# A hybrid decoder layer on one core: VectorE, ScalarE and SyncE held to the program's order, with work moved between chunks and the attention's probabilities turned by DMA

## The chip, the cores and the metric

The kernel runs on one core of a Trainium2 chip. The metric is the device time of one execution in microseconds, from repeated runs. One execution was profiled; its trace gives the start and length of every instruction on TensorE (PE, with its weight loads as PEld), VectorE (DVE), ScalarE (ACT) and GpSimd (POOL), and of the DMAs, which SyncE (SP) issues for the most part.

## The reference

One layer over 256 tokens of width 2048, in float32. What matters of it:

```python
hn = rmsnorm(h, norm_mix_w)
q, k, v, g_ret, xr, yr, g_a, g_b = split(hn @ w_in)
ret_out = silu(g_ret) * head_groupnorm(chunkwise_retention(rotary(q), rotary(k), v))   # 8 heads
xr = causal_dwconv(xr, rnn_conv_w, rnn_conv_b)                                       # 4 taps
rnn_out = gelu(yr) * rg_lru(xr, ...)       # gates by 16 small products, then a scan over tokens
merged = sigmoid(g_a) * (ret_out @ w_proj_ret) + sigmoid(g_b) * (rnn_out @ w_proj_rnn)
h = h + merged @ w_mix_out
# cross-attention over 256 memory tokens, 4 heads of 512
p = softmax((rmsnorm(h) @ w_q) @ (rmsnorm(mem) @ w_k).T * 512 ** -0.5)
h = h + (p @ (rmsnorm(mem) @ w_v)) @ w_o
# gated feed-forward, 3-tap causal convolution on 2 x 5632 channels
gate, val = split(causal_dwconv(rmsnorm(h) @ w_up, conv_w, conv_b))
h = h + (silu(gate) * val) @ w_down
out = rmsnorm(h, final_norm_w)
```

## The kernel before, in words

**Weights in chunks.** All weight matrices are laid out in one array in the order of their use. A chunk is up to four k-tiles of 128 rows by 512 columns (1 MB). `prefetch` loads a chunk into one of three `raw` buffers (SP, L244) and splits it in two halves of two k-tiles: ACT casts the high part `hi` (L269) and DVE subtracts it to get the low part `lo` (L270). There are six `hi` and six `lo` buffers, three chunks' worth. Each float32 product is three float32r matmuls: high by high, low by high, high by low. In `steps_n` a chunk is 24 matmuls of 512 columns; `chunks` keeps two chunks split ahead (`AHEAD`), so that the split of chunk c+3 is written after the matmuls of chunk c and before those of chunk c+1. It reuses chunk c's buffers.

**Work due after a chunk.** Everything that is not a weight matmul is hung on the chunks. `later(n, fn)` puts a function on a list, and `chunks` runs it n+1 chunks on, right behind that chunk's matmuls (called the boundary of the chunk below). A block of 512 output columns takes four chunks. Behind its last chunk come its drains: `turned_rows` scales the result from PSUM (DVE, L404, or L402 without a scale), and `by_dma` turns it so that features lie on partitions: ACT writes two planes of 16-bit words (L380, `pl`), SP issues two DMA transposes (L382, `pt`), and `join`, due `wait`+1 chunks later, puts the words together again (ACT, L391, `f`) and calls the function that uses them.

**The order.** The matmuls are pinned to the order of the program (`mm`, L206, and `turn_small`, L209, call `keep_in_program_order`). The instructions of ACT, DVE and SP are not: a planner orders each engine's queue by priority and by when it reckons an instruction to be ready. `high_priority` moves drains and planes forward.

**The stages, in time.** Two groups of retention (q, k, two v and two gate blocks each; rotary tables and rotations between; then per head scores, values and group norm, and `normalise` after the fourth head). Four blocks of the recurrent branch: an xr block, turned, joined and convolved by `conv_x` (ACT L763, DVE L765, three per tile), then a yr block whose join calls `gelu_y`; `recur` runs in two halves `RG_WAIT` chunks after the convolution: small products, four activations per tile (L730 to L733), and in the second half a square root (L745, which needs another activation table, as the next tanh at L787 does), a product (L746) and four scans (L748); `split_pair` (L423, L424) makes the parts for the next product. Then the gated projections, the mix-out, the attention (per head a key and a query block, `softmax`; `transpose_probs` turns the probabilities on PE; then per head a value block and `attend`), the output projection, and eleven pairs of gate and value blocks with three groups of down projections. `finish` and `last_down` end it with the final norm.

## Time and profile before

| | |
|---|---|
| median of 3 runs | 2023.56 us (2022.26 to 2023.94) |
| the profiled execution | 2022.28 us, of which its span is 2020.5 us |
| granted PE clock, mean | 0.996 |
| busy: PE, PEld, DVE, ACT | 2002.3, 1666.2, 1264.3, 1246.0 us |
| matmuls of the weights (L206, `acc`) | 8648 of 9060 |
| casts L269, mean of one | 710 of 1.052 us |
| subtractions L270, mean of one | 710 of 1.223 us |
| planes L380, joins L391, mean of one | 114 of 1.05 us, 114 of 1.35 us |
| transposes L382, issue to landing | 3.1, 4.9, 7.3 us (least, median, most) |
| DMA | 421.99 MB, 209 GB/s |

Times are in microseconds from the first instruction unless a line says ns. A group of instructions is named by line, engine, operation, and the tiles it writes and reads. A bracket behind an instruction in the timeline is the time that its engine sat idle before it, and what ended that. Matmuls are pipelined and their ends are modelled, so neighbouring ones overlap in the rows; their starts are 0.227 us apart where PE runs without a gap. Two instructions that follow each other on ACT or DVE overlap a little too, so that a row of several is shorter than the sum of its means.

### The profile page before, as it was taken

The page shows a single profiled execution, that of the slowest core. Times are in us where ns is not written, and L with a number is a line of the kernel's source. Part 1 is how long each engine was busy: PE and PEld are TensorE (multiplying, and loading weights), DVE is VectorE, ACT ScalarE, POOL GpSimd, SP SyncE. Part 2 cuts the span into 40 slices and gives each one's busy share as a digit, 9 for nine tenths or more (in the row PEclk, how much of TensorE's full clock was granted, in tenths as well). Part 3 has the DMA queues.
Part 4 walks back from the last instruction along what each step waited for, and adds up shares of the span by engine and source line. Part 5 has one row for each costly group of instructions (what it writes and reads, how often), then busy time and mean ns, then how long its engine had stood idle before and what let it go on. Part 6 is the DMA issues. An engine that isn't in the chain of part 4 may idle for free.

```text
span 2020.5 us, 23630 instructions
## 1 busy us (share of the span) xinstructions
PE 2002.3 (99%) x9060; PEld 1666.2 (82%) x9060; DVE 1264.3 (63%) x1563; ACT 1246.0 (62%) x1502; POOL 7.7 (0%) x12
## 2 busy tenths in 40 slices
PE   9999999999999999999999999999999999999998
PEld 7888888888888888788888888888888888888887
DVE  5856756888645555456555554567675577664675
ACT  6546547989434555478666556666774566644763
POOL 0000000000000000000000000000000000000000
PEclk9999999999999999999999999999999999999999
DMA  8665656665555566777766546667666566655663
GB/s 304 225 210 173 234 199 192 228 213 188 208 188 190 197 204 214 259 225 242 219 198 204 182 167 208 209 189 218 228 203 232 193 195 214 227 215 198 210 228 125
DMA packets 185153, 421.99 MB, mean 209 GB/s; under 512 B 127440, under 2 KB 132176, under 8 KB 139984
## 3 DMA queue, kind: packets, MB, share of 16 engines
q1 hardware_dynamic: 183520, 417.85, 62.2%
q10 hardware_dynamic: 1520, 2.63, 0.4%
q8 instruction: 71, 1.16, 0.2%
q14 instruction: 42, 0.34, 0.1%
HBM read 388.46 MB, written 2.10 MB: 193 GB/s over the span
## 4 chain that ended last, share of the span: by engine, by line
PE 97%; ACT 1%; DVE 1%; DMA 1%; issue 1%; SPq 0%; POOL 0%; POOLq 0%; DVEq 0%; ACTq 0%
PE acc L206 94%; PE sm L206 3%; DMA raw<-in_wall 1%; DVE lo L270 0%; ACT f L391 0%; DVE xr L765 0%; ACT pl L380 0%; ACT rows L653 0%; ACT hi L269 0%; POOL ro L507 0%; PE sm L209 0%; SPq L244 0%; DVE s L447 0%; ACT nat L1034 0%; DVE rows L404 0%
## 5 line engine op out<-in xcount | busy, mean ns | idle before, releaser
L206 PE MATMUL acc<-hi,s 128*128 128x512 f32 (+1 forms) x5680 | 1741.6, 388 | 4.2 <-ACT s L423 4.0
L270 DVE TENSOR_TENSOR lo<-raw,hi 128x1024 fp32r<-128x1024 f32 (+1 forms) x714 | 861.1, 1220 | 662.4 <-ACT hi L269 636.5
L206 PEld LDWEIGHTS acc<-hi,s 128*128 128x128 f32 x5680 | 1062.5, 188 | 222.1 <-ACT s L423 4.5
L206 PE MATMUL acc<-lo,s 128*128 128x512 f32 (+1 forms) x2840 | 1100.8, 388 | 2.0 <-DVE lo L270 2.0
L269 ACT CAST hi<-raw 128x1024 fp32r<-128x1024 f32 (+1 forms) x712 | 736.0, 1051 | 535.4 <-PE acc L206 466.7
L206 PEld LDWEIGHTS acc<-lo,s 128*128 128x128 f32 x2840 | 533.7, 188 | 111.6 <-DVE lo L270 2.7
L391 ACT COPY f<-pt 128x1024 uint16<-128x1024 uint16 x114 | 146.5, 1350 | 68.8 <-DMA pt<-pl 68.6
L380 ACT COPY pl<-rows 128x1024 uint16<-128x1024 uint16 x90 | 89.8, 1046 | 66.1 <-DVE rows L404 58.2
L404 DVE TENSOR_SCALAR rows<-acc,ro 128x512 f32<-128x512 f32 x68 | 47.8, 747 | 2.4 <-PE acc L206 2.4
L957 DVE SCALAR_TENSOR_TENSOR fv<-f,pf,fv 128x255 f32<-128x255 f32 (+1 forms) x88 | 35.8, 479 | 0.7 <-ACT fv L955 0.7
L957 DVE SCALAR_TENSOR_TENSOR fg<-f,pf,fg 128x255 f32<-128x255 f32 (+1 forms) x88 | 35.6, 478 | 0.0
L955 ACT ACTIVATE fv<-f,pf 128x256 f32<-128x256 f32 x44 | 22.9, 596 | 0.0
L955 ACT ACTIVATE fg<-f,pf 128x256 f32<-128x256 f32 x44 | 22.9, 594 | 0.0
L423 ACT ACTIVATE s<-fo 128x512 fp32r<-128x512 f32 x22 | 13.6, 635 | 14.1 <-DVE fo L977 14.1
L380 ACT COPY pl<-nat 128x1024 uint16<-128x1024 uint16 x16 | 16.0, 1046 | 9.6 <-DVE nat L835 9.6
L765 DVE SCALAR_TENSOR_TENSOR xr<-f,pa,xr 128x255 f32<-128x255 f32 (+2 forms) x48 | 20.1, 481 | 2.1 <-ACT xr L763 2.0
L446 ACT ACTIVATE s<-f,pb 128x256 fp32r<-128x256 f32 x48 | 20.4, 501 | 0.0
L447 DVE SCALAR_TENSOR_TENSOR s<-f,pb,s 128x256 fp32r<-128x256 f32 x48 | 19.9, 480 | 0.0
L206 PEld LDWEIGHTS sm<-s,s 128*128 128x128 f32 x144 | 18.8, 191 | 0.9
L206 PE MATMUL acc<-s,hi 128*128 128x512 f32 x64 | 17.6, 413 | 1.0 <-DVE hi L267 1.0
L206 PE MATMUL sm<-s,s 128*128 128x256 f32 (+1 forms) x144 | 18.6, 279 | 0.0
L421 DVE TENSOR_TENSOR s<-f,s 128x512 fp32r<-128x512 f32 x16 | 10.3, 687 | 10.0 <-ACT s L420 10.0
(154 smaller groups left out, 630.0 us busy)
## 6 DMA issues: line engine op xcount, KB each, us to landing
raw<-in_wall SPq DMA_DIRECT2D x352, 1024.0 KB, 4.9
raw<-in_wall SPq DMA_DIRECT2D x6, 512.0 KB, 6.4
nat<-in_x ACTq DMA_DIRECT2D x4, 512.0 KB, 8.2
nat<-in_x SPq DMA_DIRECT2D x4, 512.0 KB, 5.7
nat<-in_mem SPq DMA_DIRECT2D x4, 512.0 KB, 9.0
xt<-in_mem_t SPq DMA_DIRECT2D x8, 256.0 KB, 3.7
pt<-pl SPq DMA_TRANSPOSE x114, 4.9
xt<-in_x_t SPq DMA_DIRECT2D x7, 256.0 KB, 6.3
```

The source lines that it names most:

```text
L206: tc.keep_in_program_order(pe.matmul(*a, **k))
L269: act.copy(hi[:, ds], raw[:, cs, :])
L270: dve.tensor_tensor(out=lo[:, ds], in0=raw[:, cs, :], in1=hi[:, ds].bitcast(F32), op=ALU.subtract)
L380: act.copy(planes[:, :, h, :], words[:, h])
L391: act.copy(halves_[:, h], turned_[:, h])
L404: dve.tensor_scalar_mul(rows[:, tt, :], a[:, tt, :], r[:, tt : tt + 1])
L423: act.mul(t[:, :, 0:S], src, scale)
L446: act.activation(t[:, j, 0:S], src[:, j, :], AF.Identity, scale=wcol(j))
L447: dve.scalar_tensor_tensor(out=t[:, j, S:BW], in0=src[:, j, :], scalar=wcol(j), in1=t[:, j, 0:S].bitcast(F32), op0=ALU.mult, op1=ALU.subtract,
L765: dve.scalar_tensor_tensor(out=y[:, s:S], in0=z[:, 0 : S - s], scalar=p_cw(3 - s, t), in1=y[:, s:S], op0=ALU.mult, op1=ALU.add,)
L955: act.activation(y, z[:, j, :], AF.Identity, scale=pf[:, 2, t : t + 1], bias=pf[:, 3, t : t + 1])
L957: dve.scalar_tensor_tensor(out=y[:, s:S], in0=z[:, j, 0 : S - s], scalar=pf[:, 2 - s, t : t + 1], in1=y[:, s:S], op0=ALU.mult, op1=ALU.add,)
```

## The change

A small class passes every call on to an engine and pins the instruction behind everything that was written before it on that engine. PE, and from the end of the first q block on ACT, DVE and SP, are wrapped in it:

```diff
+class InOrder:
+    def __init__(self, tc, engine):
+        self.tc, self.engine = tc, engine
+    def __getattr__(self, name):
+        f = getattr(self.engine, name)
+        return lambda *a, **k: self.tc.keep_in_program_order(f(*a, **k))
...
+    pe = InOrder(tc, pe)
...
     qjoin = [joined(t, "q") for t in next(q_steps)]
     assert next(q_steps, None) is None
+    act, dve, sp = (InOrder(tc, e) for e in (act, dve, sp))
     later(0, tables)
```

The loads of the raw chunks are written where their buffer is read for the last time, right behind the split of the chunk three before:

```diff
+    def load(n):
+        while len(raws) < min(n, len(stream)):
...
+            raw = wp.tile([P, KC, BW], F32, tag="raw", bufs=RAW_BUFS, name=nm("raw"))
+            raws.append((raw, src))
+            if i >= 2 * len(EARLY):
+                sp.dma_start(out=raw[:, 0:nk, :], in_=src)
...
             ahead.append(((row, c), parts))
+            if i >= 2 * len(EARLY):
+                load(i + 1 + RAW_BUFS)
```

Work is moved between boundaries. The recurrence starts one chunk sooner (`RG_WAIT` 3 to 2) and the last gelu too. In `normalise`, the scaling and turning of the rows is put off to the next two boundaries. In `gelu_y` the two halves are interleaved and the product with the scan's result goes to the next boundary (`times_y`); the same is done with the last split of `gate_up`. In `residual` the turning comes before the squares, and the memory's sums of squares are spread over four boundaries:

```diff
-RG_WAIT = 3
+RG_WAIT = 2
...
+            def two_heads(i):
+                rows = big([P, 2, BW], s="rows")
+                for hh in (2 * i, 2 * i + 1):
...
+                        act.mul(rows[:, tt, c : c + DV], raws[hh][:, tt, :], rstd[:, hh, tt : tt + 1])
+                by_dma(rows, words.append, 4)
+            for i in range(2):
+                later(i, lambda i=i: two_heads(i))
...
+    def times_y(f, xr):
+        for pr in range(2):
+            o = tmp("rn")
...
+            dve.tensor_tensor(out=o, in0=xr[:, cs, :], in1=f[:, cs, :], op=ALU.mult)
+            rnn.append(split_pair(o, 0.5))
...
+            for y, y2, th in halves_:
                 act.activation(th, y2, AF.Tanh)
                 dve.scalar_tensor_tensor(out=y, in0=th, scalar=1.0, in1=y, op0=ALU.add, op1=ALU.mult)
+            later(0, lambda: times_y(f, xr[0]))
...
-        turned_rows(gemm_n("w_in", 0, xs, NT, O_YR + b * BW), rs0, gelu_y, 4 if b < 3 else 3)
+        turned_rows(gemm_n("w_in", 0, xs, NT, O_YR + b * BW), rs0, gelu_y, 4 if b < 3 else 2)
...
             dve.tensor_add(h, h, gemm_n(w, 0, st, NT, b * BW))
+            by_dma(hrow[b], lambda f, b=b: turn(f, b, out, wcol))
             squares(h, ss, b)
-            by_dma(hrow[b], lambda f, b=b: turn(f, b, out, wcol))
...
-                sum_squares(mnat[c], ss, c)
-            rsms.append(rstd_rows(ss))
+                later(c, lambda c=c: sum_squares(mnat[c], ss, c))
+            later(4, lambda: rsms.append(rstd_rows(ss)))
...
-            hid.append(split_pair(o, 0.5))
+            rows.append(o)
+        later(0, lambda: hid.extend(split_pair(o, 0.5) for o in rows))
```

The probabilities of two heads share one tile and are turned by `by_dma` when the second is done; the sixteen PE transposes and four copies from PSUM are gone:

```diff
-        later(1, lambda: transpose_probs(pr_))
+        if b % 2 == 1:
+            by_dma(probs[-1], lambda f: pTs.extend(f[:, 2 * i : 2 * i + 2, :] for i in range(2)))
```

More of the change, by code (lines that the diff above doesn't have):

```diff
@@ L203, in hybrid_layer @@
         pe.matmul(warm[:, 0, 0:P], ones, ones, start=True, stop=True)
-    def mm(*a, **k):
-        tc.keep_in_program_order(pe.matmul(*a, **k))
-    def turn_small(*a):
-        tc.keep_in_program_order(pe.transpose(*a))
+    pe = InOrder(tc, pe)
     plan = weight_plan()
@@ L226, in hybrid_layer @@
     at = [0]
+    raws = []
+    def load(n):
+        while len(raws) < min(n, len(stream)):
+            i = len(raws)
+            nk = stream[i][2]
+            size = nk * P * BW
+            src = wall[at[0] : at[0] + size].rearrange("(p k n) -> p k n", p=P, k=nk)
+            at[0] += size
+            raw = wp.tile([P, KC, BW], F32, tag="raw", bufs=RAW_BUFS, name=nm("raw"))
+            raws.append((raw, src))
+            if i >= 2 * len(EARLY):
+                sp.dma_start(out=raw[:, 0:nk, :], in_=src)
     def prefetch(n):
@@ L232, in prefetch @@
             taken[0] += 1
-            size = nk * P * BW
-            src = wall[at[0] : at[0] + size].rearrange("(p k n) -> p k n", p=P, k=nk)
-            at[0] += size
-            raw = wp.tile([P, KC, BW], F32, tag="raw", bufs=RAW_BUFS, name=nm("raw"))
+            load(i + 1)
+            raw, src = raws[i]
             k2 = row // (KH * P)
@@ L242, in prefetch @@
                 xs.load(k2 + 1)
-            for a, b in zip(cuts, cuts[1:]):
+            for a, b in zip(cuts, cuts[1:]) if early else ():
                 sp.dma_start(out=raw[:, a:b, :], in_=src[:, a:b, :])
@@ L329, in steps_t @@
                         a, sx = a[:, S:BW], sx[:, 0:S]
-                    mm(
+                    pe.matmul(
                         a, part, sx, start=k == 0 and t == 0, stop=k == nk - 1 and t == 0, skip_group_check=True
@@ L342, in products_n @@
         l = sx[:, S + tt * P : S + (tt + 1) * P]
-        mm(o, h, hi, start=start, stop=False)
-        mm(o, l, hi, start=False, stop=False)
-        mm(o, h, lo, start=False, stop=stop)
+        pe.matmul(o, h, hi, start=start, stop=False)
+        pe.matmul(o, l, hi, start=False, stop=False)
+        pe.matmul(o, h, lo, start=False, stop=stop)
     def steps_n(w, row, st, nk, col):
@@ L365, in product @@
         for i, (a, b) in enumerate(((l[0], r[0]), (l[0], r[1]), (l[1], r[0]))):
-            mm(o, a, b, start=start and i == 0, stop=stop and i == 2, skip_group_check=True)
+            pe.matmul(o, a, b, start=start and i == 0, stop=stop and i == 2, skip_group_check=True)
     def halves(t, j, cs=slice(0, S)):
@@ L478, in products @@
                 cs = slice(tt * P, (tt + 1) * P)
-                mm(bc[:, cs], ones, diag[:, cs], start=True, stop=True)
+                pe.matmul(bc[:, cs], ones, diag[:, cs], start=True, stop=True)
             act.copy(rsb, bc)
@@ L640, in normalise @@
         def normalise():
-            rows = [big([P, 2, BW], s="rows") for _ in range(2)]
             rstd = rsqrt_small(stats[:, :, 1], 8, 1.0, GN_EPS).rearrange("p (h t) -> p h t", t=2)
@@ L652, in normalise @@
                     )
-                    act.mul(rows[hh // 2][:, tt, (hh % 2) * DV : (hh % 2 + 1) * DV], y, rstd[:, hh, tt : tt + 1])
-            for i, r in enumerate(rows):
-                by_dma(r, words.append, 2 + i)
+            def two_heads(i):
+                rows = big([P, 2, BW], s="rows")
+                for hh in (2 * i, 2 * i + 1):
+                    for tt in range(2):
+                        c = (hh % 2) * DV
+                        act.mul(rows[:, tt, c : c + DV], raws[hh][:, tt, :], rstd[:, hh, tt : tt + 1])
+                by_dma(rows, words.append, 4)
+            for i in range(2):
+                later(i, lambda i=i: two_heads(i))
         for hh in range(4):
@@ L727, in recur @@
             for i in range(2):
-                mm(gp[:, i, :], rgw[:, i, j, :], xr[:, j, :], start=True, stop=True)
+                pe.matmul(gp[:, i, :], rgw[:, i, j, :], xr[:, j, :], start=True, stop=True)
             tr = tp.tile([P, S], F32, tag="tr", bufs=2, name=nm("tr"))
@@ L750, in recur @@
             )
+    def times_y(f, xr):
+        for pr in range(2):
+            o = tmp("rn")
+            cs = slice(2 * pr, 2 * pr + 2)
+            dve.tensor_tensor(out=o, in0=xr[:, cs, :], in1=f[:, cs, :], op=ALU.mult)
+            rnn.append(split_pair(o, 0.5))
     for b in range(4):
@@ L780, in gelu_y @@
         def gelu_y(f, xr=xr):
-            for pr in range(2):
-                y = f[:, 2 * pr : 2 * pr + 2, :]
-                y2, th = tmp("y2"), tmp("yt")
+            halves_ = [(f[:, 2 * pr : 2 * pr + 2, :], tmp("y2"), tmp("yt")) for pr in range(2)]
+            for y, y2, _ in halves_:
                 act.activation(y2, y, AF.Square)
@@ L786, in gelu_y @@
                 dve.tensor_tensor(out=y2, in0=y2, in1=y, op=ALU.mult)
+            for y, y2, th in halves_:
                 act.activation(th, y2, AF.Tanh)
                 dve.scalar_tensor_tensor(out=y, in0=th, scalar=1.0, in1=y, op0=ALU.add, op1=ALU.mult)
-            for pr in range(2):
-                o = tmp("rn")
-                cs = slice(2 * pr, 2 * pr + 2)
-                dve.tensor_tensor(out=o, in0=xr[0][:, cs, :], in1=f[:, cs, :], op=ALU.mult)
-                rnn.append(split_pair(o, 0.5))
+            later(0, lambda: times_y(f, xr[0]))
         turned_rows(gemm_n("w_in", 0, xs, NT, O_XR + b * BW), rs0, conv_x)
-        turned_rows(gemm_n("w_in", 0, xs, NT, O_YR + b * BW), rs0, gelu_y, 4 if b < 3 else 3)
+        turned_rows(gemm_n("w_in", 0, xs, NT, O_YR + b * BW), rs0, gelu_y, 4 if b < 3 else 2)
     def gated(c0, w, st, b, o):
@@ L870, in hybrid_layer, with softmax @@
     dve.tensor_scalar_mul(lscale, rstd_rows(ss1), float(XD**-0.5))
-    pTs, done = [], [0]
-    def softmax(q, k):
+    pTs, probs = [], []
+    def softmax(b, q, k):
         lg = small()
@@ L884, in softmax @@
         dve.scalar_tensor_tensor(out=nb, in0=mx, scalar=-1.0, in1=lscale, op0=ALU.mult, op1=ALU.mult)
-        pr_ = tmp("prob")
+        if b % 2 == 0:
+            probs.append(big([P, 2, BW], s="prob"))
+        pr_ = probs[-1][:, :, (b % 2) * S : (b % 2 + 1) * S]
         for tt in range(2):
@@ L893, in softmax @@
             dve.tensor_scalar_mul(pr_[:, tt, :], pr_[:, tt, :], rsm[:, tt : tt + 1])
-        later(1, lambda: transpose_probs(pr_))
-    def transpose_probs(pr_):
-        t = small()
-        for kt in range(2):
-            for tt in range(2):
-                turn_small(t[:, kt, tt * P : (tt + 1) * P], pr_[:, tt, kt * P : (kt + 1) * P], ident)
-        if done[0] == len(pTs):
-            two = tp.tile([P, 2, BW], F32, tag="sig", bufs=2, name=nm("pT"))
-            pTs.extend(two[:, i, :].rearrange("p (k s) -> p k s", s=S) for i in range(2))
-        pT = pTs[done[0]]
-        done[0] += 1
-        act.copy(pT, t)
+        if b % 2 == 1:
+            by_dma(probs[-1], lambda f: pTs.extend(f[:, 2 * i : 2 * i + 2, :] for i in range(2)))
     def split_block(f):
@@ L916, in query @@
             qs = split_block(f)
-            later(1, lambda: softmax(qs, ks))
+            later(1, lambda: softmax(b, qs, ks))
         turned_rows(gemm_n("xa_w_q", 0, h1s, NT, b * BW), None, query)
@@ L971, in gate_up @@
     def gate_up(gt, vl, hid):
+        rows = []
         for pr in range(2):
```

## The prediction

> **What bounds the kernel now.** I read the page's totals first, then the chain that ended last, then who TensorE (PE) waited for after the start, then the PE clock around the one long wait, then the timelines of the recurrent stage.

> ```profile
> span 2020.5 us, 23630 instructions
> PE 2002.3 (99%) x9060; PEld 1666.2 (82%) x9060; DVE 1264.3 (63%) x1563; ACT 1246.0 (62%) x1502; POOL 7.7 (0%) x12
> PE 97%; ACT 1%; DVE 1%; DMA 1%; issue 1%; SPq 0%; POOL 0%; POOLq 0%; DVEq 0%; ACTq 0%
> ```

> PE sets the time, and its stream is pinned already. One chunk of four k-tiles (24 matmuls) is this piece of the chain in order of time (start, length, what), 5.44 us without the last matmul's overhang:

> ```profile
> 300.96 5.47 PE acc L206 x24
> ```

> The waits of PE from 60 us to the end (total, times, longest) are two lines, 6.0 us. A fixed order can win those and little else:

> ```profile
> PE acc L206 <- ACT s L423: 4.0, 1, 4.0
> PE acc L206 <- DVE lo L270: 2.0, 1, 2.0
> ```

> A wait costs more than its length. The first matmuls after the long one, in the timeline, and the busy times of two stretches (length, then PE, PEld, DVE, ACT, POOL, then granted clock, DMA share, GB/s):

> ```profile
> 846.35 1.52 PE L206 MATMUL acc<-hi,s 128*128 128x512 f32 x2 [4.04 <-ACT s L423]
> ```
> ```profile
> 846.35:850.60 4.25, 4.25 (x9) 3.11 (x10) 1.27 (x2) 0.47 (x1) 0.00 (x0) 0.50 1.07 412
> 340.30:344.00 3.70, 3.69 (x16) 3.08 (x17) 2.22 (x2) 3.70 (x4) 0.00 (x0) 1.00 0.93 190
> ```

> After the 4.04 us wait the granted clock was 0.50 for 4.25 us, 2.1 us lost; after the 1.98 us wait, which ends at 340.3, it was 1.00. So I charge 2.1 us more for an idle above 4 us and nothing below 2. [...]

> The stage with least air on the other engines is the recurrent one (340 to 530 us: ACT busy 160.23 of 190 us, DVE 155.79). Its durations, here and below, from ACT and then DVE:

> ```profile
> 403.80 1.28 ACT L745 ACT_TABLE_LOAD   x1
> 405.09 1.06 ACT L745 ACTIVATE tt<-tt 128x1024 f32<-128x1024 f32 x1
> 407.95 1.99 ACT L380 COPY pl<-rows 128x1024 uint16<-128x1024 uint16 x2
> 423.74 2.56 ACT L391 COPY f<-pt 128x1024 uint16<-128x1024 uint16 x2
> 426.32 2.08 ACT L763 ACTIVATE xr<-f,pa 128x256 f32<-128x256 f32 x4
> 428.31 1.99 ACT L269 CAST hi<-raw 128x1024 fp32r<-128x1024 f32 x2
> ```
> ```profile
> 409.22 2.43 DVE L748 TENSOR_TENSOR_SCAN xr<-aa,ti 128x256 f32<-128x256 f32 x4
> 411.57 2.33 DVE L270 TENSOR_TENSOR lo<-raw,hi 128x1024 fp32r<-128x1024 f32 x2
> 421.37 1.29 DVE L792 TENSOR_TENSOR rn<-xr,f 128x512 f32<-128x512 f32 x2
> 428.27 1.41 DVE L404 TENSOR_SCALAR rows<-acc,ro 128x512 f32<-128x512 f32 x2
> 429.59 3.23 DVE L765 SCALAR_TENSOR_TENSOR xr<-f,pa,xr 128x253 f32<-128x253 f32 x8
> ```

> **The rule that the new order makes.** The split of chunk c+3 (casts L269, subtractions L270) is written behind everything due after chunk c. Its buffers come free as chunk c ends, and PE needs it two chunks later. Whatever is due at boundary c, with every hand-over between ACT and DVE, is now queued ahead of a split with 10.9 us of air. Before, the splits were slipped in between.

> **The recurrent stage, blocks 1 to 3.** Time 0 is the end of the xr block's last chunk. DVE comes late: the previous block's second recurrence half has its products 10.88 us earlier, and behind them stand eight activations (3.5), the table load (1.28), the square root (1.0), the product L746 (1.2), the scans (2.4) and two splits' subtractions (4.6), 14.05 with hand-overs, so DVE is free at 3.2. Then in order: rows L404 to 4.6; planes L380 to 6.6; casts of split 3 to 8.5; yr's join L391 to 11.0; squares to 12.1; table load to 13.4; two tanh to 14.6; casts of split 4 to 16.5; xr's join to 18.9; the first convolution step on ACT to 19.5; twelve L765 on DVE (0.395 apart) to 24.3; times_y, four hand-overs of about 0.65 between DVE and ACT, to 27.5; first cast of split 5 to 28.6, its subtraction 29.8. While ACT's scaling in times_y waits for DVE, the casts of split 5 stand behind it, and PE behind those. PE wants the split at 4 x 5.44 = 21.8: 6.85 us idle, 0.4 waiting for the subtraction, 2.1 at half clock. That is 9.3 a block, 27.9 for three. Bounds: ACT's own work in this stretch, with no hand-over at all, is 19.2 us and starts at 4.6, so it ends 2.0 past the deadline (2.9 with the subtraction, 8.7 for three); with no late DVE it would end in time. I take 27.9, since the hand-overs are real dependencies.

> **Other places, in time order,** each by the same adding of rows. Rotary tables, both q rotations and the first v split stand before split 12: ready at 66.2 and 67.45 instead of 61.0: 5.2 + 0.4 + 2.1 = 7.75. First retention group: the q join, a rotation and two_heads fall on one boundary, then the second rotation and a v split: 1.2 + 2.15 = 3.35. Same in block 0 of the recurrence: 0.2. Gelu of block 3, moved to wait 2, then times_y and the gate's tanh: 2.45. Softmax of head 3, two planes, the v split and a weight split all stand before attend(0)'s cast and subtraction, which PE needs at once: 4.6, with part of it cold 5.4 (4.6 to 6.7). Last block: finish(2)'s squares and products stand before the last split, 24 narrow matmuls of 0.12 ahead of need: 2.3. Together with the 27.9: 49.35. Each of these I let go down to half.

> **What goes.** The 4.04 us wait at 842 us with its 2.1: in the trace the join L391 (843.12) stands behind a cast that waits for PE (842.17); written order puts it ahead of an earlier split, and planes, then transposes landing in 3.2, then join and split end about 1 us in time. The 1.98 at 340 us, where spreading two_heads is what helps, and 0.38 at 930. The 16 PE transposes, 0.44 us per head on the chain: 1.76. Together 10.27.

> **What I cost at nothing.** The probabilities' new path adds four planes copies (1.05 each), four joins (1.35) and four transposes to SP (1.3 each) and drops four copies (0.58); head 1's and 3's planes sit before the drain at the same boundary, and without head 3 (counted above) the split behind still ends about 2 before PE's need. Raw loads are queued behind those transposes on SP, but each is issued as soon as its buffer is read, three chunks ahead (16 us against 4.9 to land). Squares moved behind the planes, sums of squares spread, words joined four chunks later: each 1.5 to 2.5 us on a boundary with over 2.5 spare. Feed-forward: a gate and value pair takes 43.5 us; with transposes complete about 6.5 and 4.7 us after the planes (the two values that alternate there, from the planes' end to the join), DVE's in-order loop is 43.4 long. That cover is thin: 1 us more of landing costs up to 2 us a pair once 2 to 3 us of slack are used.

> **Sum.** 49.35 - 10.27 = +39.1. The profiled run took 2022.28 (1.78 outside its span): 2061.4. The median of the runs is 1.28 above it: 2062.7, forecast 2062.

> **Rivals.**
> Faster: the three engines reach a boundary early, because most functions due there don't wait for PE, and every split is ready. Then only the 10.27 goes: 2013.3. Place: split 5 of each recurrent block; it decides from 28.6 coming down to 21.8. For it: at 842 the planner's own choice lost time, and ACT averages only 84% in this stage. Against: 19.2 us of ACT work alone miss the deadline by 2. Chance 0.15.
> Smaller: DVE is not late at xr's end, so each block loses 4.3 with no half clock (3 x 5.0 less): 2048. For it: half clock and lateness come from my chain alone. Against: scans and both splits are rows. 0.12.
> Feed-forward gives way: both transposes need 7.3 us, the longest landing seen, so each pair falls 3.3 us behind, 11 pairs, less 3 us of slack in each of three parts: +27, 2089. For: landings are 3.1 to 7.3, median 4.9. Against: DMA is busy 64% there, and SP gets its loads earlier. 0.14.
> Nothing changes because the planner's queues were in this order already: 2023.6. Against: L435 at 67.52 and 69.99 has two casts between, which written order forbids. 0.04.
> My forecast: 0.55.

> **How the numbers follow.** Low 2032: three blocks at 8.7 and the other places at half (10.7 of 21.45), less 10.27, is +9, or 2033; high 2090 takes in the feed-forward rival. That leaves out the faster and the unchanged cases, 0.19. A measurement here tells 0.2% (4 us) from none: faster 0.15, same 0.04, slower 0.81.

> **What would show it.** Right: PE waits for L269 and L270 appear, about 7 us long, three times at about 47 us distance in the recurrent stage, one near 61 us, one after the first v block of the attention; PEclk falls below 0.95 there; the wait at 842 is gone; ACT shows idle before L423 and L269 released by DVE L765 and L792. Wrong: PE idle in the recurrent stage under 5 us in all; or most of the new idle in the feed-forward part, behind DMA pt. A span within 4 us of 2020.5 with the waits moved would refute the sum, not the rule.

## The result, and the profile after

The changed kernel took 2077.1 us (median of 4 runs, 2075.0 to 2078.4), the kernel before 2023.4 us beside it: ratio 1.0265, 95% interval 1.0247 to 1.0283, 2.7% slower. The profiled execution took 2076.0 us with a span of 2074.2, 53.7 more than before.

The page of the changed kernel, its span, its busy times and its chain by engine. Every pinned instruction is recorded with the wrapper's line, L138, so groups must be told apart by their tiles:

```profile
span 2074.2 us, 23528 instructions
PE 2016.9 (97%) x9044; PEld 1670.2 (81%) x9044; DVE 1279.3 (62%) x1563; ACT 1241.8 (60%) x1506; POOL 8.3 (0%) x12
PE 83%; ACT 6%; DVE 5%; DMA 3%; issue 2%; SPq 0%; POOL 0%; POOLq 0%; ACTq 0%; DVEq 0%
```

PE's share of the chain fell from 97% to 83%; ACT and DVE now hold 11% where they held 2%, with almost the same work: DVE has the same 1563 instructions (busy 15 us longer in all), ACT four more (busy 4 us less). The four largest groups of waits of PE from 60 us to the end (total, times, longest) say for what:

```profile
PE acc L138 <- ACT hi L138: 32.1, 10, 7.6
PE acc L138 <- DVE lo L138: 4.9, 8, 1.0
PE sm L138 <- ACT ps L138: 4.5, 1, 4.5
PE sm L138 <- DVE ps L138: 3.0, 4, 1.0
```

`hi` and `lo` are the two parts of a weight split, `ps` the two parts of a head's probabilities, `sm` a small result in PSUM. The wait for `s` of 4.0 is gone, 45 us of others have come. The longest in PE's timeline (start of the work that follows the wait, its length, what, and in brackets the wait):

```profile
398.37 1.22 PE L138 MATMUL acc<-hi,s 128*128 128x512 f32 x2 [7.55 <-ACT hi L138]
454.57 1.22 PE L138 MATMUL acc<-hi,s 128*128 128x512 f32 x2 [7.19 <-ACT hi L138]
511.65 1.22 PE L138 MATMUL acc<-hi,s 128*128 128x512 f32 x2 [7.20 <-ACT hi L138]
1178.47 0.58 PE L138 MATMUL sm<-ps,v 128*128 128x256 f32 x1 [4.46 <-ACT ps L138]
2049.02 0.50 PE L138 MATMUL acc<-hi,s 128*128 128x256 f32 x2 [1.55 <-ACT hi L138]
```

The first three are recurrent blocks 1 to 3. Why ACT was late, in ACT's timeline of block 2:

```profile
429.48 2.00 ACT L138 COPY pl<-rows 128x1024 uint16<-128x1024 uint16 x2 [5.88 <-DVE rows L138]
...
443.88 2.08 ACT L138 ACTIVATE xr<-f,pa 128x256 f32<-128x256 f32 x4
450.97 0.63 ACT L138 ACTIVATE s<-rn 128x512 fp32r<-128x512 f32 x1 [5.01 <-DVE rn L138]
452.96 0.63 ACT L138 ACTIVATE s<-rn 128x512 fp32r<-128x512 f32 x1 [1.36 <-DVE rn L138]
453.49 3.87 ACT L138 CAST hi<-raw 128x1024 fp32r<-128x1024 f32 x4
```

ACT stands idle for 5.0 and 1.4 us in front of `times_y`, because DVE is at its twelve convolution steps. Behind it, at 453.49, are four casts of weights that wait for nothing but their turn. PE needed the first at 447.38. In the same stretch on DVE the convolution is one piece:

```profile
444.51 5.82 DVE L138 SCALAR_TENSOR_TENSOR xr<-f,pa,xr 128x255 f32<-128x255 f32 x12 [1.70 <-ACT xr L138]
```

Busy times of stretches (length, then PE, PEld, DVE, ACT, POOL, then granted clock, DMA share, GB/s) show what else a wait costs; the second row begins inside the wait that ends at 454.57:

```profile
340.00:540.00 200.00, 176.97 (x747) 143.83 (x746) 143.56 (x188) 151.32 (x201) 0.00 (x0) 0.93 0.59 182
449.40:459.70 10.30, 5.09 (x11) 3.59 (x12) 8.63 (x11) 5.03 (x6) 0.00 (x0) 0.50 0.14 48
```

In the recurrent stage PE lost 22.7 us of its 199.7, and the clock was 0.93; after this one wait 5.1 us of work ran at half clock, 2.6 us lost.

**Where the 53.7 us arose.** PE's matmuls into `acc` are the same 8648 in the same order in both kernels, so the delay of each one can be followed through the span, waits and clock together:

| place | predicted | measured |
|---|---|---|
| start of the kernel | 0 | -1.2 |
| rotary tables, first v split | +7.75 | +6.2 |
| first retention group | +3.35 | +6.4 |
| recurrence, block 0 | +0.2 | +1.1 |
| the wait at 340 | -1.98 | -1.98 |
| recurrence, blocks 1 to 3 | +27.9 | +30.2 |
| gelu of block 3 | +2.45 | +1.65 |
| the wait at 842 and its half clock | -6.15 | -6.5 |
| mix-out, 860 to 985 | -0.38 | +4.7 |
| 16 transposes of PE | -1.76 | -1.2 in three heads, the fourth in the next row |
| attend(0) | +5.4 | +7.45 |
| attend(1) to attend(3) | 0 | +2.7 |
| feed-forward | 0 | 0 |
| last block | +2.3 | +4.2 |
| sum | +39.1 | +53.7 |

### The profile page after: what moved, and what is told of

Read it like the earlier page. It is cut to its first block, busy times and chain, and to the rows that moved or that the text cites. A ratio compares the mean times of both kernels' runs of the same rounds, so it can differ in the third digit from the quotient of the medians.

```text
span 2074.2 us, 23528 instructions
## 1 busy us (share of the span) xinstructions
PE 2016.9 (97%) x9044; PEld 1670.2 (81%) x9044; DVE 1279.3 (62%) x1563; ACT 1241.8 (60%) x1506; POOL 8.3 (0%) x12
## 4 chain that ended last, share of the span: by engine, by line
PE 83%; ACT 6%; DVE 5%; DMA 3%; issue 2%; SPq 0%; POOL 0%; POOLq 0%; ACTq 0%; DVEq 0%
PE acc L138 81%; PE sm L138 2%; DVE lo L138 2%; ACT hi L138 2%; DMA raw<-in_wall 1%; DVE xr L138 1%; ACT f L138 1%; DMA nat<-in_x 1%; ACT pl L138 0%; DMA posi<-in_positions 0%; ACT tt L138 0%; ACT L138 0%; ACT s L138 0%; DVE nat L138 0%; DVE rows L138 0%
## 5 line engine op out<-in xcount | busy, mean ns | idle before, releaser
L138 PE MATMUL acc<-hi,s 128*128 128x512 f32 (+1 forms) x5680 | 1748.7, 389 | 32.7 <-ACT hi L138 32.1
L138 PEld LDWEIGHTS acc<-hi,s 128*128 128x128 f32 x5680 | 1066.7, 189 | 254.5 <-ACT hi L138 36.1
L138 PE MATMUL acc<-lo,s 128*128 128x512 f32 (+1 forms) x2840 | 1105.6, 389 | 5.2 <-DVE lo L138 4.9
L138 DVE TENSOR_TENSOR lo<-raw,hi 128x1024 fp32r<-128x1024 f32 x694 | 819.0, 1221 | 405.8 <-ACT hi L138 392.5
L138 ACT CAST hi<-raw 128x1024 fp32r<-128x1024 f32 x694 | 696.1, 1048 | 275.8 <-PE acc L138 257.4
L138 PEld LDWEIGHTS acc<-lo,s 128*128 128x128 f32 x2840 | 536.1, 189 | 121.1 <-DVE lo L138 11.2
L138 ACT COPY pl<-rows 128x1024 uint16<-128x1024 uint16 x90 | 89.7, 1044 | 169.1 <-DVE rows L138 168.9
L138 ACT COPY f<-pt 128x1024 uint16<-128x1024 uint16 x118 | 151.2, 1350 | 39.1 <-DMA pt<-pl 39.1
L138 DVE SCALAR_TENSOR_TENSOR fv<-f,pf,fv 128x255 f32<-128x255 f32 x88 | 39.6, 481 | 31.4 <-ACT fv L138 29.9
L138 DVE TENSOR_SCALAR rows<-acc,ro 128x512 f32<-128x512 f32 x68 | 47.8, 744 | 13.5 <-PE acc L138 13.4
L138 DVE SCALAR_TENSOR_TENSOR fg<-f,pf,fg 128x255 f32<-128x255 f32 x88 | 39.6, 482 | 26.1 <-ACT fg L138 24.5
L138 DVE TENSOR_TENSOR nat<-nat,acc 128x1024 f32<-128x1024 f32 (+1 forms) x23 | 24.9, 1080 | 46.7 <-PE acc L138 46.7
L138 ACT COPY pl<-nat 128x1024 uint16<-128x1024 uint16 x16 | 16.0, 1044 | 33.4 <-DVE nat L138 33.4
L290 DVE TENSOR_TENSOR lo<-raw,hi 128x1024 fp32r<-128x1024 f32 (+1 forms) x20 | 21.9, 1117 | 11.9 <-ACT hi L289 11.5
L138 DVE SCALAR_TENSOR_TENSOR s<-f,pb,s 128x256 fp32r<-128x256 f32 x48 | 20.2, 482 | 13.1 <-ACT s L138 13.1
L138 ACT ACTIVATE sig<-acc,half_rs 128x512 f32<-128x512 f32 x16 | 10.1, 685 | 29.9 <-PE acc L138 29.9
L138 DVE SCALAR_TENSOR_TENSOR xr<-f,pa,xr 128x255 f32<-128x255 f32 (+2 forms) x48 | 22.1, 482 | 6.2 <-ACT xr L138 5.1
L138 ACT ACTIVATE junk<-nat 128x512 f32<-128x512 f32 x30 | 18.6, 622 | 11.1 <-DVE nat L138 11.1
L138 ACT COPY pl<-m 128x1024 uint16<-128x1024 uint16 x8 | 8.0, 1044 | 28.5 <-DVE m L138 28.5
L138 DVE SCALAR_TENSOR_TENSOR v<-acc,ro,v 128x512 fp32r<-128x512 f32 x16 | 12.0, 750 | 20.9 <-ACT v L138 20.9
L138 ACT ACTIVATE prob<-sm,sx,lscale 128x256 f32<-128x256 f32 x8 | 4.5, 561 | 34.2 <-DVE sx L138 34.2
L138 DVE TENSOR_TENSOR s<-f,s 128x512 fp32r<-128x512 f32 x16 | 10.4, 689 | 22.3 <-ACT s L138 22.3
```

The costliest lines, as they stand in the source:

```text
L138: return lambda *a, **k: self.tc.keep_in_program_order(f(*a, **k))
L290: dve.tensor_tensor(out=lo[:, ds], in0=raw[:, cs, :], in1=hi[:, ds].bitcast(F32), op=ALU.subtract)
```

## The experiments

**Without the fixed order.** The changed kernel, less one line:

```diff
-    act, dve, sp = (InOrder(tc, e) for e in (act, dve, sp))
```

> The changed kernel without the pins on ACT, DVE and SP (PE stays pinned; loads, moved work and the turning by DMA stay). Theory A (the written order makes the waits: a split stands behind all that is due at its boundary): the three waits of about 7.2 us in the recurrent stage, the 3.7 us at 69 us and the 4.5 us at 1178 us go, PE idle after 60 us under 8 us in all, time 2010 to 2026. Rival B (the moved work or the probabilities' new path costs the time by itself): PE idle stays over 30 us, time over 2060. Rival C (the loads, now issued right behind a split, are what is late): the waits stay but fall to the raw transfers.

2031.7 us (2031.0 to 2032.8), ratio 1.0046 (1.0029 to 1.0063). So about 45 of the 53.7 us come from the fixed order of the three engines, and all three recurrent waits of 7 us are gone. The two largest groups of PE's waits from 60 us to the end:

```profile
PE acc L138 <- DVE lo L290: 5.3, 4, 2.0
PE acc L138 <- ACT s L445: 4.0, 1, 4.0
```

But the rest of the change is no gain either, 8.9 us slower than before: above the expected range. The place of it was followed in the same way: the 340 wait is gone, but two waits of 1.8 and 2.0 us for lo came near 380; the 4.04 us wait at 842 is still there; about 5 us arise at the first attend, about 3 in the feed-forward behind three waits (0.65 for `s`, 0.3 and 1.2 for lo). The wait at 842 is thus cured by the fixed order, not by the moved work. Why the two waits near 380 came stays open.

**The fixed order without the moved work.** The kernel before with the wrappers on all engines, and the early `load`, and nothing else of the change:

> The kernel before with the pins on PE, ACT, DVE and SP and the loads written behind the splits, and nothing else: no work moved, probabilities turned on PE. Theory A: worse than the changed kernel, since gelu and the product with the scan stand on one boundary and the recurrence one chunk later leaves DVE about 8.6 us late at the end of an xr block instead of 3.2: over 10 us of idle a block there, and the first retention group's normalise on one boundary; time 2085 to 2130. Rival B (the moved work costs the time): near 2024, at most 2035.

2123.8 us (2120.8 to 2124.8), ratio 1.0497 (1.0481 to 1.0513), inside the theory's range. The waits of PE from 60 us to the end:

```profile
PE acc L138 <- ACT hi L138: 48.3, 16, 6.8
PE acc L138 <- DVE lo L138: 15.2, 14, 3.0
```

Fixing the order costs 101 us on the old program, and the moved work takes 47 of them away again. As a whole the moved work is worth something only under the fixed order; in the planner's order (above) it and the probabilities together cost 9, though one part of it gains there, as a run below shows.

**The recurrence one chunk earlier still.**

```diff
-RG_WAIT = 2
+RG_WAIT = 1
```

> The changed kernel with the recurrence one more chunk earlier (RG_WAIT 1). Theory A says DVE comes 3.2 us late to an xr block's end because of the recurrence just before; one chunk earlier takes that away: idle before chunk 5 of recurrent blocks 1 to 3 falls from 7.2 to about 4 us each, and 1.7 us of small products may hide in it; time 2060 to 2069. Rival D (ACT's own load in this stretch is the bound, the late DVE does not matter): waits stay within 1 us of 7.2, time 2075 to 2079.

2078.2 us (2075.0 to 2078.9), ratio 1.0271 (1.0256 to 1.0286): no gain. The time is the rival's, but its sign is not there: it had the waits stay within 1 us of 7.2. DVE is no longer late: its rows now wait for PE. But the loss only splits in two; in PE's timeline of one block:

```profile
423.80 0.54 PE L138 MATMUL acc<-lo,s 128*128 128x512 f32 x1 [3.10 <-DVE lo L138]
457.27 0.73 PE L138 MATMUL acc<-hi,s 128*128 128x512 f32 x2 [3.09 <-ACT hi L138]
```

The next hi wait ends at 514.60, 57.3 us after this one; in the changed kernel the distance is 57.1 (511.65 less 454.57), in the kernel before a block takes 47.0 (the same two matmuls at 427.19 and 474.19). The chain that ended last lies wholly on PE over such a block of the kernel before. Over a block of the changed kernel (454 to 512 us) it lies on PE for 29% of the time, on ACT and DVE, in turn, for 65%; here (457 to 515) for 12% and 80%. So a chain of hand-overs between ACT and DVE sets most of the block's length, and in this placing it is as long as in the changed kernel.

**Two products one chunk later.** `times_y`, and `attend` of each head, come after the next split:

```diff
-            later(0, lambda: times_y(f, xr[0]))
+            later(1, lambda: times_y(f, xr[0]))
...
-        later(0, lambda b=b, v=v: attend(b, v))
+        later(1, lambda b=b, v=v: attend(b, v))
```

> The changed kernel with times_y one boundary later and attend one boundary later. Theory A: in the recurrent stage split 5 no longer stands behind the four hand-overs of times_y, but split 6 does: each of blocks 1 to 3 loses about 5 us instead of 10; at the attention the waits of 4.46 and 0.95 us and the three of 0.67 go, about 10 us; time 2044 to 2058. Rival D (ACT's load is the bound in the recurrent stage): the wait there only moves, 28 us and more stay in the three blocks; time 2065 to 2070.

2065.0 us (2063.5 to 2067.1), ratio 1.0210 (1.0194 to 1.0225): short of the theory's range by 7 us, at the lower end of the rival's. By the delays the recurrent stage with its last gelu got about 6 us back, the attention about 5. With `times_y` out of the way the cast came at 445.95, before PE needed it. The wait stayed, though, half as long, and changed sides (PE, then DVE):

```profile
451.61 0.79 PE L138 MATMUL acc<-lo,s 128*128 128x512 f32 x1 [3.83 <-DVE lo L138]
```
```profile
444.60 5.82 DVE L138 SCALAR_TENSOR_TENSOR xr<-f,pa,xr 128x255 f32<-128x255 f32 x12 [1.68 <-ACT xr L138]
450.33 2.35 DVE L138 TENSOR_TENSOR lo<-raw,hi 128x1024 fp32r<-128x1024 f32 x2
```

The subtraction of that split stands behind the convolution. Two queues have to be right for one split. A block takes 55.7 us here (this wait ends at 451.61, the next at 507.32): moving this piece shortens the chain by 1.4, not more.

**Which engine's queue?** The changed kernel with VectorE, and then with ScalarE, left to the planner:

```diff
-    act, dve, sp = (InOrder(tc, e) for e in (act, dve, sp))
+    act, sp = (InOrder(tc, e) for e in (act, sp))
```

> The changed kernel (2077.1 us) with VectorE left to the planner; ScalarE and SyncE stay in the program's order. Theory A (the 45 us of the fixed order come from the hand-overs between ScalarE and VectorE: a split needs a cast on the one and a subtraction on the other, and in a fixed order both stand behind a step that goes to and fro between the two, so both must be free before a split can pass it): ScalarE's casts still stand behind the two scalings of the recurrent block's product, so each of blocks 1 to 3 gets at most 1 to 2 us better; some of the tables and of attend(0) comes back: 2064 to 2077, and PE's waits in the recurrent stage stay over 4 us and are still for hi. Rival B (one engine's queue alone makes the loss, and it is VectorE's, which comes late into each recurrent block by about 3 us and runs the twelve convolution steps in one piece): nearly all 45 us come back: 2030 to 2045.

2057.1 us (2056.6 to 2058.0), ratio 1.0168 (1.0152 to 1.0183).

```diff
+    dve, sp = (InOrder(tc, e) for e in (dve, sp))
```

> The changed kernel (2077.1 us) with ScalarE left to the planner; VectorE and SyncE stay in the program's order. Theory A (both engines must be free before a split can pass): the casts can pass the scalings, but the subtraction of the same split stands on VectorE behind the twelve convolution steps and the products, so PE's waits in the recurrent stage turn from hi into lo and keep most of their length; what stands on ScalarE alone (tables, attend(0)) gets up to 8 us shorter: 2060 to 2075. Rival C (it is ScalarE's queue alone, the engine with the casts and all copies): 2030 to 2045.

2077.9 us (2076.3 to 2079.8), ratio 1.0270 (1.0255 to 1.0285). The wait of PE in block 2 in the two, VectorE free and ScalarE free:

```profile
441.12 0.79 PE L138 MATMUL acc<-lo,s 128*128 128x512 f32 x1 [4.03 <-DVE lo L290]
```
```profile
457.24 0.79 PE L138 MATMUL acc<-lo,s 128*128 128x512 f32 x1 [6.68 <-DVE lo L138]
```

Freeing ScalarE gives nothing: hi waits of 7.2 to 7.6 become lo waits of 6.7 to 8.3, since DVE's fixed order still holds the subtraction. Freeing VectorE gives 20 us, of which about 11 in blocks 1 to 3, and still leaves 4 us in each block. Both rivals in which one engine's queue makes the whole loss fall. The theory's own ranges were missed as well, by 3 us on ScalarE, which gains nothing at all, and by 7 on VectorE, which gains more: of the two, VectorE's order is the dearer. With VectorE free the theory also had the wrong half: it said that the waits would still be for hi, and they are for lo. ACT, then DVE, in block 2:

```profile
434.85 3.88 ACT L138 CAST hi<-raw 128x1024 fp32r<-128x1024 f32 x4
```
```profile
432.46 4.55 DVE L802 SCALAR_TENSOR_TENSOR xr<-f,pa,xr 128x255 f32<-128x255 f32 x11 [0.76 <-ACT xr L138]
439.84 6.90 DVE L290 TENSOR_TENSOR lo<-raw,hi 128x1024 fp32r<-128x1024 f32 x6
```

The first cast was done at 435.9, before PE wanted it; the planner itself laid the subtraction behind the convolution.

**The recurrent stage alone left to the planner**, on all three engines; the rest stays fixed:

```diff
+    act, dve, sp = nc.scalar, nc.vector, nc.sync
     for b in range(4):
         rgw = big([P, 2, 4, P], s="rgw")
...
+    act, dve, sp = (InOrder(tc, e) for e in (act, dve, sp))
     def gated(c0, w, st, b, o):
```

> The changed kernel (2077.1 us) with VectorE, ScalarE and SyncE left to the planner in the recurrent stage alone (from the first recurrent block to the gated products); everywhere else their order stays fixed. Theory A: the 30.2 us of blocks 1 to 3 and the 1 to 2 us of blocks 0 and 3 go, and the 3 us that the unpinned kernel lost near 380 come: 2046 to 2051. Rival I (the loss sits in what the change moved in this stage, the recurrence's wait of two and the products put off, not in the fixed order): 2065 to 2077.

2053.4 us (2049.0 to 2056.2), ratio 1.0150 (1.0137 to 1.0164), the median 2.4 above the range. The waits of 7 us in blocks 1 to 3 are gone, two for lo near 390 (1.97 and 2.00, as in the first experiment) have come; by the delays the stage gave 24 us back. So the fixed order, not the work that was moved in this stage, makes the loss there, and of these runs only the ones with both engines free undo it. SyncE was free in them too; its order alone was not tested, but between 380 and 515 us of the changed kernel ACT never waits for a load.

**The probabilities alone**, both ways round. First the changed kernel with PE's transposes back:

```diff
-        if b % 2 == 1:
-            by_dma(probs[-1], lambda f: pTs.extend(f[:, 2 * i : 2 * i + 2, :] for i in range(2)))
+        later(1, lambda: transpose_probs(pr_))
```

> The changed kernel (2077.1 us) with the attention's probabilities turned on TensorE again, as before; all else is kept. Theory A: attend(0)'s cast loses two planes copies (2.1 us) ahead of it, the 16 transposes on PE come back (1.76 us): 2076 to 2079, nothing that can be measured. Rival E (the way through the DMA is itself what makes attend(0) wait, 7.45 us here): the waits at 1178 and at the three attends after it go, 10 us less and 1.8 more: 2069.

2074.5 us (2073.5 to 2075.9), ratio 1.0254 (1.0238 to 1.0269): 2.6 us below the changed kernel, between the two expectations, but not clear of noise: the changed kernel's interval, 1.0247 to 1.0283, overlaps. In the profiled executions PE lost 7.4 us over the attention here, against the kernel before, and 8.4 in the changed kernel. PE's wait for the first `ps` is 1.44 us instead of 4.46, but the later attends still wait 0.67 each. Then the kernel before with the DMA turn:

> The kernel before (2022.8 us) with one part of the change alone: the probabilities turned by DMA, two heads at a time; no engine's order fixed. Theory A with what the unpinned kernel's trace showed (the planes copies of heads 2 and 3, 2.0 us, at the planner's highest priority, ran ahead of the first v block's drain, and PE waited for v four times, 3.0 us in all, at 1136 to 1140): the same here, about 4.5 us at that place less 1.3 to 1.8 for the 16 transposes that PE no longer does: 2025 to 2027. Rival F (what cost time in the unpinned kernel is something else, as the moved products and the new wait of the recurrence): only the transposes go: 2021.

2025.8 us (2023.6 to 2027.8), ratio 1.0015 (1.0005 to 1.0024): 2.7 us slower, as expected. ACT's timeline there:

```profile
1129.67 1.99 ACT L380 COPY pl<-prob 128x1024 uint16<-128x1024 uint16 x2 [0.88 <-DVE prob L895]
1131.57 1.04 ACT L269 CAST hi<-raw 128x1024 fp32r<-128x1024 f32 x1
1132.52 0.68 ACT L435 ACTIVATE v<-acc,ro 128x512 fp32r<-128x512 f32 x1
```

The planes copy of two heads goes ahead of the first v block's drain, for which PE waits. By the delays PE saves 1.9 us in the four heads, by the transposes it no longer does, and loses 5.5 at this place, most of it in four waits for `v`, 3.0 us in all. In the planner's order this part of the change costs 2.7 us, and the transposes were cheaper on PE; under the fixed order the runs do not settle its size.

**Fixing the order only where it pays.** The kernel before; ACT and DVE in the program's order only from the last block of the retention's projection to the first block of the mix-out:

```diff
+    def pin(on):
+        nonlocal act, dve
+        act, dve = (InOrder(tc, e) if on else e for e in (nc.scalar, nc.vector))
...
     for b in range(4):
+        if b == 3:
+            pin(True)
         m = gated(O_GA, "w_proj_ret", ret, b, big([P, 2, BW], s="m"))
...
                 steps(b)
+                if b == 1:
+                    pin(False)
```

> The kernel before (2022.8 us) with ScalarE and VectorE fixed to the program's order in one place only: from the last block of the retention's projection to the end of the first block of the mix-out product. Nothing else is changed. Theory A (a fixed order pays where the planner put a step behind a cast that waits for PE, and costs where ScalarE and VectorE hand over to each other with little air): the 4.04 us wait at 842 goes with its half-clock phase, 6.15 us as in the changed kernel: 2016 to 2017. Rival G (a place where the order is fixed pushes what is written after it, as the squares and planes of the first mix-out block): half is given back at 860 to 935: 2019 to 2021.

2023.1 us (2022.1 to 2025.7), ratio 1.0002 (0.9993 to 1.0011): no difference, so both expected ranges were missed. The wait at 842 went, and with its half clock over PE was 5.8 us ahead at 852; at 935 all was given back. ACT's timeline, a stretch, and SyncE's timeline (start, time to issue, what):

```profile
852.38 2.00 ACT L138 CAST hi<-raw 128x1024 fp32r<-128x1024 f32 x2 [10.71 <-DMA raw<-in_wall]
```
```profile
844.00:850.00 6.00, 6.00 (x28) 4.99 (x27) 0.00 (x0) 0.00 (x0) 0.00 (x0) 1.00 1.06 408
```
```profile
834.15 2.12 SPq L193 DMA_DIRECT2D nat<-in_x  x4
836.32 2.49 SPq L193 DMA_DIRECT2D nat<-in_mem  x4
838.91 20.68 SPq L255 DMA_DIRECT2D raw<-in_wall  x5
```

ACT and DVE have nothing to do for those 6 us and the DMA engines are full, at 408 GB/s: eight row loads of the mix-out, 0.52 MB each, stand on SyncE ahead of the weights. They arrive when they can, however early PE is. The changed kernel shows the same line at 894.00, with the same 10.71, and 2.2 of its +4.7 us in the mix-out come right behind it, at 903. The rest comes between 970 and 983, most of it behind a wait of ACT for another load (the transposed memory tokens, `xt`, 3.76 us). No run spread the loads in the changed kernel, so that these loads take back most of its 6.5 is inferred.

**The same, and the retention's rows two heads at a time** (`normalise` as in the change):

> As the run with the order fixed from the last retention block to the first mix-out block alone, and also the retention's rows written two heads at a time, with their joins four chunks later. Theory A: the 1.98 us wait at 340 goes as it did in the unpinned kernel, about 2 us less than the other: 2014 to 2015. Rival H (the planner lays the recurrent stage anew when rows move, and the waits of 1.8 and 2.0 us at 380 in the unpinned kernel come from that): 2016 to 2019, with waits for lo near 380.

2018.2 us (2016.4 to 2020.4), ratio 0.9980 (0.9971 to 0.9989): the time is the rival's, but its sign is absent. The wait at 340 is gone, no wait came near 380, so the two waits in the first experiment are not from this part. The gain, 4.9 us over the last, is larger than the 1.94 us wait it removes; in the profiled executions a stretch of half clock went with that wait, and a second one at 931, 1.7 us each (the mean granted clock is 0.999 here, 0.998 in the run before this one); the first of them is shown under the hardware.

**And the eight row loads spread over three blocks:**

```diff
-    hrow = [load_rows(x, c) for c in range(4)]
-    mnat = [load_rows(mem, c) for c in range(4)]
+    hrow, mnat = [load_rows(x, 0)], []
...
     def memory_steps(b):
-        if b == 1:
+        if b < 3:
+            hrow.append(load_rows(x, b + 1))
+        if b < 2:
+            mnat.extend(load_rows(mem, c) for c in (2 * b, 2 * b + 1))
+        if b == 2:
```

> As the run with the order fixed in one place and the retention's rows spread (2018.2 us), and also the eight row loads of the mix-out (four of x, four of mem, 0.52 MB each, issued together just after 829 us) written out over three blocks: one of x ahead of the projection, two of mem and one of x at the start of each of blocks 0 and 1, the last of x at block 2; the squares of mem move from block 1 to block 2. Theory K (what the removed wait at 842 gave was given back because the weights' loads stand behind those eight on SyncE: the DMA engines were full, share 1.00 to 1.06 from 832 to 850, and ScalarE waited 10.7 us for a raw chunk): that wait falls below 4 us, PE's two waits near 861 (0.63 and 0.53) go, those near 923 (0.93 and 1.29) go or halve: 2014 to 2016. Rival L (it is ScalarE's own load, the squares and planes at these boundaries, not the loads): the waits stay or move to block 2: 2018 to 2020.

2013.4 us (2013.0 to 2014.1), ratio 0.9954 (0.9940 to 0.9967), faster than both kernels, and the waits near 861 and 923 went. From 852 to 940 us the run before this one gave back 4.6 us, this one nothing. Its page, and the wait of ACT for the same raw chunk:

```profile
PE 1998.2 (99%) x9060; PEld 1663.6 (83%) x9060; DVE 1264.3 (63%) x1563; ACT 1241.7 (62%) x1502; POOL 7.7 (0%) x12
```
```profile
842.53 2.00 ACT L138 CAST hi<-raw 128x1024 fp32r<-128x1024 f32 x2 [3.96 <-DMA raw<-in_wall]
```

ACT's wait was 10.45 us in the run before this one; that it fell is the doing of the loads alone. The edit also takes the squares of mem off the boundary in front of 861, where they stood ahead of the late split, so what the loads and what the squares cost PE there is not separated; at their new place the squares make PE wait for nothing.

From 60 us to the tail PE waits once, 0.61 us. The 9.5 us gained are the two waits of before with what hung on them, and the way to them was to fix the order over some 65 us of the program, not all of it, and to spread two groups of copies and loads.

## Why the prediction was right, and where it was not

**The rule** (a split stands behind everything due at its boundary) held in each place that was named. What was to show it is there: hi waits near 7 us three times, one near 61 (it ends at 68.99), one at the first attend, a clock under 0.95 in the stage, the wait at 842 gone, ACT idle before `times_y` by DVE. Only the distance of the three was said wrongly, 47 us; each wait adds to it, and it is 56 to 57. The two signs of being wrong did not come: PE idled 22.7 us in the recurrent stage, not under 5, and none of the new idle lies in the feed-forward.

**The recurrent blocks**: 30.2 us against 27.9. Counted from the end of xr's last chunk, the chain said DVE free at 3.2, planes from 4.6, the convolution's first step on ACT from 18.9, the first cast of split 5 done at 28.6, PE's need at 21.8. In the trace of block 2, where the next gemm's first matmul starts at 425.46, it is 2.6, 4.0, 18.4, 29.1 (453.49 and 1.06 for one cast) and 21.9. DVE came 0.6 earlier than said, and the way from the planes to that cast took 25.1 us where 24.0 were counted.

**The rival Smaller** laid 4.3 us a block to DVE's lateness. In the changed kernel DVE was late, by 2.6 us. The run with the recurrence a chunk earlier took the lateness away and gained nothing. The term was part of the chain and no separate cause.

**The clock term** was mis-sized, and with it the step that charges nothing for a wait below 2 us. The first retention group's wait was 2.26 us, the last block's 1.55 and 0.76, and half clock followed in both places (0.50 from 213.9 to 217.3 and from 2050.3 to 2053.7), 1.5 and 1.7 us lost. The rest of the 6.4 against 3.35 and the 4.2 against 2.3 was not taken apart. The 2.1 itself was read from a row that ends at 850.60; the half clock lasted until 851.1, 4.75 us of work and 2.4 lost, and 2.6 in block 2 of the changed kernel. How short waits and the clock went together in the traces is told below.

**Attention**: 7.45 against 5.4, and 2.7 more in attend(1) to attend(3), for which nothing was charged. The three waits of 0.67 us for DVE's `ps` belong to a cast and a subtraction that PE needs at once behind each v split. The probabilities' way itself was costed at nothing apart from head 3; in the planner's order it costs 2.7 us net, with the transposes already taken off, and under the fixed order its size is not settled.

**What goes** came out as said: at 842 by the mechanism given (in written order the join runs ahead), at 340 because the rows are written two heads at a time, as the run with that part alone shows. The step that failed is what was costed at nothing behind it, the raw loads on SyncE. They were weighed against the turns, not against the eight row loads that stand in front of them in the mix-out. So 4.7 of the 6.5 us were given back within 140 us, 2.2 of them right behind the late weights.

**Feed-forward** was charged nothing, and its thin cover held: the delay is the same at its start and its end. The rival in which it gives way fell, as did the one in which the engines reach a boundary early and the one in which nothing changes.

The median was 15 us above the forecast and inside the range, which was 58 us wide. The mechanism carried it; the sum was low because its errors mostly point one way. Nearly all of it are these terms: 2.3 in the recurrence, 3.1 and 1.9 in the first retention group and the last block, where the clock was charged nothing, 4.8 in the attention, 5.1 in the mix-out, less 1.2 at the start and 1.6 at the tables.

## What to carry to other kernels

An order fixed over the whole program made, out of the steps that go to and fro between two engines, a chain longer than PE's time per block, and a split that needs both engines was late as long as either queue held it: count the chain's length against PE's time per block, and fix the order only where the trace shows a step queued behind one that waits. Where a wait is removed, look at once at what arrives next and from which queue; here the loads behind it took the gain back until they were spread. A saving of 0.44 us per head on the engine that bounds was not worth 2 us of copies, at the wrong place, on the engine that feeds it.

## What the runs showed of the hardware

```profile
335.70:339.10 3.40, 2.63 (x12) 1.85 (x10) 3.40 (x10) 3.40 (x5) 0.00 (x0) 1.00 0.00 0
339.10:342.50 3.40, 2.19 (x10) 1.81 (x11) 3.40 (x4) 3.40 (x4) 0.00 (x0) 1.00 0.67 127
342.50:345.90 3.40, 3.40 (x17) 2.92 (x16) 1.55 (x3) 3.40 (x6) 0.00 (x0) 1.00 0.88 229
```
```profile
337.40:340.80 3.40, 1.46 (x7) 1.02 (x6) 3.40 (x6) 3.40 (x4) 0.00 (x0) 1.00 0.39 73
340.90:344.20 3.30, 3.30 (x9) 2.58 (x8) 1.48 (x2) 3.30 (x4) 0.00 (x0) 0.50 0.98 225
```

In the first the wait is shared by two stretches, 0.8 and 1.2 us, and the clock stays; in the second it lies in one, and 1.7 us more are lost. From the first the prediction had read that such a wait costs no clock.

**A burst on the DMA engines that no mean shows.** In the run with the order fixed in one place they moved 363 GB/s from 838 to 844 and 408 from 844 to 850, at busy shares of 1.00 and 1.06, beside a mean of 209 over the span of the kernel before; the eight row loads are 4.2 MB. Six microseconds at such a rate occur elsewhere too (in the kernel before 419 GB/s from 210.5 and 414 from 485, at 1.02 and 1.01, with 0.63 and 0.16 in the six behind), without a wait of PE; what sets this burst apart from those two is its length, with the weights behind it.
